# Weights repacked in load order, and the last expert pair of a two-layer MoE trunk summed in PSUM

## The chip, the core and the metric

The kernel runs on one core of one Trainium2 chip. The metric is device time in microseconds (us) of one execution. Engines are named PE (TensorE), DVE (VectorE), ACT (ScalarE), POOL (GpSimd) and SP (SyncE, which here only issues DMAs). All times in the text are from one profiled execution unless it says otherwise.

## What is computed

A trunk of two layers over 256 tokens of width 1024, all in float32. Each layer has a mixer sub-layer and a mixture of 32 experts, both modulated by six vectors that a matrix `w_ada` makes out of one conditioning vector; a final RMS norm ends it. Cut to what matters here:

```python
mod = silu(c) @ w_ada[l] + b_ada[l]                  # sh1, sc1, g1, sh2, sc2, g2
h = modulate(rms_norm(x, mixer_norm_g[l]), sh1, sc1)
x = x + g1 * (mixed(h @ w_in[l]) @ w_out[l])         # conv and pooling branches inside
h2 = modulate(rms_norm(x, ffn_norm_g[l]), sh2, sc2)  # top-1 group, top-2 experts in it
for e in range(32):                                  # combine[:, e] is 0 for tokens not routed to e
    act = silu(h2 @ w_gate[l, e]) * (h2 @ w_up[l, e])
    x = x + g2 * ((act * combine[:, e]) @ w_down[l, e])
return rms_norm(x, final_norm_g)
```

Each weight is read once: 296 MB in all, 201 MB of it the experts' (3 MB an expert).

## The kernel before

**Weights.** `plan` writes a list of 1 MB tiles in the order of their use; `issue` walks it and lets SP issue the DMAs, in that order. A tile goes into one of 14 ring buffers (`wt`, 128 partitions x 2048 floats), or into one of up to five work buffers (`wx`, table `SPARE`) while these are not needed for other things. Each `done(key)` in the program frees a buffer and plans the next load, which waits on the chip until the buffer's last reader is through. Besides, the framework hands out eight semaphores (DMAHW0 to DMAHW7) to the DMAs of SP and ACT in turn, in the order in which the program names the DMAs: a DMA cannot be issued before the one eight places ahead of it has landed. So at most eight are under way, whatever their size.

**How a tile is read.** A `w_in` tile lies packed in DRAM and is one DMA of 1 MB, 8 KB a partition. The others are read out of the tables as the caller has them: a gate/up tile is two DMAs of 512 KB, one from the gate table and one from the up table, 4 KB a partition (L112); a tile of `w_expert_down`, `w_ada`, `w_out` or `w_conv_out` is one DMA of 1 MB in runs of 4 KB (L114); the down tiles of the last pair of a layer are two DMAs of 512 KB each.

**Experts.** `blocks` goes through 16 pairs of experts; a pair has up to 64 tokens for each expert, and the two experts stand beside each other in the 128 partitions. A pair needs six tiles: four of gate/up (key `("gu", l, expert, h)`, h being the half of the contraction) and two of down (`("ed", l, expert)`). On PE a pair is, in order: gate/up, 32 matmul instructions (L1118); the previous pair's results scattered back to the 256 tokens (`scatter`, four parts of two matmuls, L1073 and L1074, three parts ahead of the transposes and one behind); two transposes (L1133); down, 16 instructions in two halves of 512 output columns (`down`, L1093). ACT takes silu (L1126), which stands once in each pair, DVE multiplies by the routing weight (L1127) and evacuates the transposes (L1135). Then, for each half, DVE multiplies by g2 (`gain`, L1099), ACT rounds this to the short format fp32r (L1100), and DVE makes the remainder (`rest`, L1104), so that two fast matmuls give full precision in the scatter. `add` (L1081) adds a scattered part from PSUM to the token array `xs` on DVE.

**The gain of the final norm** is loaded in the second layer: at the end of pair 5 (counted from 0) ACT issues a 4 KB DMA into the tile `fz` (L1204), and after pair 9 two matmuls spread it over the partitions (L1208).

**The end.** After the last pair's down, its parts are scattered and added like the others, ACT takes the squares of `xs` (L340), POOL multiplies the left half by the gain (L1180) and takes the power -1/2 (L346), ACT and DVE scale (L1214, L1215), and SP issues four output DMAs one after the other (L1218).

## Time and profile before

| | us |
|---|---|
| median of 3 runs (lowest, highest) | 851.8 (851.02, 852.24) |
| the profiled execution, its own time | 852.07 |
| its span, first to last event of the profile | 850.2 |

The page of the profile gives PE as busy for 778.5 us, 92% of the span, and the DMA queue of SP as 89.6% of 16 DMA engines over it. Neither says which of the two is waited for: matmuls overlap in their records, and the DMA queue is often full ahead of need. That is read from the distance of one pair to the next, from the GB/s of stretches, and from the waits.

### The profile page before, as it was taken

Reading aid. Unit: us, or ns where it says so; the run is one execution under the profiler, and the core shown is the slowest. Engines: PE = TensorE matmul, PEld = TensorE weight load, DVE = VectorE, ACT = ScalarE, POOL = GpSimd, SP = SyncE. Lnnn points to the kernel's source line nnn. Section 1 sums busy time; section 2 is a strip of 40 time slices with the busy share of each in tenths; the row PEclk is TensorE's granted clock in tenths of the full one; section 3 lists DMA queues with packets and bytes.
Section 4 is the critical chain, followed back from the end, with each engine's and each line's share of the span. In section 5 each row is a group of like instructions: output and inputs, shape, how many; then the busy total and the mean of one; then the engine's idle time right before and its main releaser. Section 6 shows DMA issues by size and latency. Waiting matters only on the chain. (4 is left out here: it accounts for less than half of the span.)

```text
span 850.2 us, 11978 instructions
## 1 busy us (share of the span) xinstructions
PE 778.5 (92%) x4382; PEld 454.4 (53%) x4382; DVE 505.6 (59%) x1023; ACT 277.0 (33%) x494; POOL 198.2 (23%) x133
## 2 busy tenths in 40 slices
PE   4599999997899999999879999999779999999985
PEld 2389986755333433343349998686523333333432
DVE  2369984976344644545376997497734554544545
ACT  2254544434122222222145454543322222222212
POOL 1258972510000000000034898161000000000001
PEclk9699999999999999999989999999889999999998
DMA  9999758969999999999999954797579998999993
GB/s 358 413 421 411 270 174 333 358 238 403 393 409 408 409 410 402 409 409 409 403 417 420 381 182 149 293 385 256 193 264 366 409 405 316 408 410 408 409 408 119
DMA packets 78080, 298.39 MB, mean 351 GB/s; under 512 B 7349, under 2 KB 7861, under 8 KB 74426
## 3 DMA queue, kind: packets, MB, share of 16 engines
q1 hardware_dynamic: 77448, 296.44, 89.6%
q10 hardware_dynamic: 434, 1.06, 0.3%
q8 instruction: 37, 0.61, 0.3%
q14 instruction: 33, 0.27, 0.1%
q0 software_dynamic: 128, 0.02, 0.0%
HBM read 296.44 MB, written 1.05 MB: 350 GB/s over the span
## 5 line engine op out<-in xcount | busy, mean ns | idle before, releaser
L1118 PE MATMUL pb<-wt,XTW 128*64 128x512 f32 x872 | 219.6, 593 | 12.9 <-DMA wt<-in_w_expert_up_dram 8.2
L414 POOL TENSOR_TENSOR wlo<-wt,whi 128x1024 fp32r<-128x1024 f32 x60 | 147.3, 2466 | 88.5 <-ACT whi L412 64.8
L1118 PEld LDWEIGHTS pb<-wt,XTW 128*64 128x64 f32 x872 | 73.6, 137 | 131.3 <-issue 124.5
L1127 DVE SCALAR_TENSOR_TENSOR sl<-sl,rtile,pb 128x256 f32<-128x256 f32 x32 | 15.4, 480 | 164.4 <-ACT sl L1126 164.4
L473 DVE SCALAR_TENSOR_TENSOR pd<-vpad,cols,pd 128x256 f32<-128x256 f32 x232 | 106.9, 488 | 5.7
L412 ACT CAST whi<-wt 128x1024 fp32r<-128x1024 f32 x80 | 82.8, 1049 | 73.8 <-PE pb L352 40.8
L1093 PE MATMUL pd<-wt,aT 128*64 128x512 f32 x360 | 102.7, 618 | 1.8 <-DVE aT L1135 0.5
L1100 ACT CAST yhl<-y 128x512 fp32r<-128x512 f32 x64 | 39.6, 619 | 137.9 <-DVE y L1099 137.9
L351 PE MATMUL pa<-hhl,whi 128*128 128x256 f32 x224 | 66.7, 298 | 5.2 <-ACT hhl L386 5.2
L1126 ACT ACTIVATE sl<-pb 128x256 f32<-128x256 f32 x32 | 12.3, 385 | 172.7 <-PE pb L1118 172.7
L352 PE MATMUL pa<-hhl,whi 128*128 128x256 f32 x224 | 65.6, 293 | 0.3
L353 PE MATMUL pa<-hhl,wlo 128*128 128x256 f32 x224 | 64.5, 288 | 0.6 <-POOL wlo L414 0.6
L351 PE MATMUL pb<-hhl,whi 128*128 128x256 f32 x224 | 63.6, 284 | 0.0
L297 PE MATMUL pd<-wt,cb 128*32 128x512 f32 x384 | 51.4, 623 | 13.1 <-DMA wt<-in_w_ada_dram 13.0
L352 PE MATMUL pb<-hhl,whi 128*128 128x256 f32 x224 | 62.7, 280 | 0.0
L353 PE MATMUL pb<-hhl,wlo 128*128 128x256 f32 x224 | 62.6, 279 | 0.0
L1093 PEld LDWEIGHTS pd<-wt,aT 128*64 128x64 f32 x360 | 29.1, 141 | 59.4 <-issue 39.2
L1104 DVE TENSOR_TENSOR yhl<-y,yhl 128x512 fp32r<-128x512 f32 x64 | 44.3, 693 | 22.0 <-ACT yhl L1100 22.0
L392 POOL MEMSET vpad<- 128x120 f32 x2 | 0.4, 200 | 242.5 <-DVE sl L1127 242.5
L1118 PE MATMUL pb<-wx,XTW 128*64 128x512 f32 x152 | 55.1, 593 | 0.0
L1093 PE MATMUL pd<-wx,aT 128*64 128x512 f32 x152 | 52.7, 610 | 0.8 <-DVE aT L1135 0.5
L1099 DVE TENSOR_TENSOR y<-pd,gb 128x512 f32<-128x512 f32 x64 | 44.0, 688 | 15.4 <-PE pd L1093 15.4
(257 smaller groups left out, 1345.5 us busy)
## 6 DMA issues: line engine op xcount, KB each, us to landing
wt<-in_w_expert_gate_dram SPq DMA_DIRECT2D x109, 512.0 KB, 11.5
wt<-in_w_expert_up_dram SPq DMA_DIRECT2D x109, 512.0 KB, 12.8
wt<-in_w_ada_dram SPq DMA_DIRECT2D x48, 1024.0 KB, 13.7
wt<-in_w_expert_down_dram SPq DMA_DIRECT2D x41, 1024.0 KB, 11.7
wt<-in_w_in_dram SPq DMA_DIRECT2D x28, 1024.0 KB, 20.1
wx<-in_w_expert_down_dram SPq DMA_DIRECT2D x19, 1024.0 KB, 12.0
wx<-in_w_expert_gate_dram SPq DMA_DIRECT2D x19, 512.0 KB, 11.1
wx<-in_w_expert_up_dram SPq DMA_DIRECT2D x19, 512.0 KB, 10.2
```

Of the source, the lines that this page charges most:

```text
L297: nc.tensor.matmul(ps[j:j + 32, :], cb[:, 2 * i + a, :], halves(w[:, a, :], h), start=i == 0, stop=i == 3)
L351: nc.tensor.matmul(o, ah, bh, start=start, stop=False, skip_group_check=True)
L352: nc.tensor.matmul(o, ah, bl, start=False, stop=False, skip_group_check=True)
L353: nc.tensor.matmul(o, al, bh, start=False, stop=stop, skip_group_check=True)
L412: nc.scalar.copy(hi, wv)
L414: eng.tensor_tensor(lo, wv, hi.bitcast(F32), op=OP.subtract)
L473: nc.vector.scalar_tensor_tensor(acc[:, j, :] if t == CONV_K - 1 else a, src, w, a, op0=OP.mult, op1=OP.add)
L1093: nc.tensor.matmul(o[64 * j:64 * j + 64, :], aTs[b][:, h, 64 * j:64 * j + 64], wv[j][:, h, :], start=h == 0, stop=h == 1)
L1099: nc.vector.tensor_tensor(y, downs.pop(n), s["g2"][:, n * 512:(n + 1) * 512], op=OP.mult)
L1100: nc.scalar.copy(ys[b][0][:, n * 512:(n + 1) * 512], y)
L1104: nc.vector.tensor_tensor(yl, downs.pop(("y", n)), yh.bitcast(F32), op=OP.subtract)
L1118: nc.tensor.matmul(p[64 * j:64 * j + 64], XT[:, k, 64 * j:64 * j + 64], w[j][:, :, kk, :], start=k == 0, stop=k == KC - 1)
```

## The change

The host lays out all weights as 1 MB tiles in load order, each contiguous, 8 KB a partition: `w_gate_up` puts the gate and the up rows of a tile behind each other, `w_down`, `w_ada`, `w_out` and `w_conv_out` are packed likewise. Every tile is then one DMA. In the last pair of each layer the two gate/up tiles of h = 1 hold contraction steps 4, 5 and 6, 7 of both experts, in the place of one expert each. In the last pair of layer 1, ACT first copies `xs` into four PSUM tiles (`hold`), and the scatters of the last two pairs are accumulated on them by PE (`onto`), those of the pair before between the two halves of gate/up; the second half of the last down is done in two pieces of 256 columns whose results are scattered as plain float32, without the split into fp32r and remainder. The final norm reads PSUM (`last` takes the place of `finish`), and one of the four output DMAs is issued by ACT.

```diff
-            key, src, (a, b), q = stream[state["issued"]]
+            key, src, shape, q = stream[state["issued"]]
             t = room(key, q)
             if t is None:
                 return
-            v = t[:, :a * b].rearrange("p (a b) -> p a b", b=b)
-            if isinstance(src, tuple):
-                v = v.rearrange("p (i k) h -> p i k h", i=2)
-                for i, sr in enumerate(src):
-                    nc.sync.dma_start(out=v[:, i], in_=sr)
-            else:
-                nc.sync.dma_start(out=v, in_=src)
+            v = t[:, :src.shape[-1]]
+            nc.sync.dma_start(out=v, in_=src)
+            v = v.rearrange(*(("p (a b) -> p a b",) if len(shape) == 2 else ("p (i a b) -> p i a b",)),
+                            **dict(zip("ab" if len(shape) == 2 else "iab", shape)))
             tiles[key] = v
...
     def plan_ada(l, m, part=range(4)):
-        v = w_ada[l].rearrange("(p k) n -> p k n", k=KC)
         for i in part:
-            plan(("ada", l, m, i), v[:, 2 * i:2 * i + 2, m * D:(m + 1) * D], (2, D))
+            plan(("ada", l, m, i), w_ada[l, m, i], (2, D))
 
...
     def plan_pair(l, e):
-        ents = []
-        for h in range(2):
-            for j in range(2):
-                ents.append((("gu", l, e + j, h),
-                             tuple(w[l, e + j].rearrange("(p k) h -> p k h", k=KC)[:, 4 * h:4 * h + 4, :]
-                                   for w in (w_expert_gate, w_expert_up)), (KC, DE)))
-        wd = w_expert_down[l, e:e + 2].rearrange("e (j p) n -> p e j n", p=P)
-        for j in range(2):
-            if e + 2 < NE:
-                ents.append((("ed", l, e + j), wd[:, j], (2, D)))
-            else:
-                ents.append((("ed", l, e + j), tuple(wd[:, z, :, 512 * j:512 * j + 512] for z in range(2)), (4, 512)))
+        ents = [(("gu", l, e + j, h), w_gate_up[l, e + j, h], (4, 2, DE) if h and e + 2 == NE else (2, 4, DE))
+                for h in range(2) for j in range(2)]
+        ents += [(("ed", l, e + j), w_down[l, e + j], (2, D) if e + 2 < NE else (2, 2, 512)) for j in range(2)]
...
+        def gate_up(b, p, XT, h):
+            w = need(*(("gu", l, 2 * b + j, h) for j in range(2)))
+            for kk in range(4):
+                k = 4 * h + kk
+                for j in range(2):
+                    wv = w[kk // 2][:, 2 * j:2 * j + 2, kk % 2, :] if h and b == nb - 1 else w[j][:, :, kk, :]
+                    nc.tensor.matmul(p[64 * j:64 * j + 64], XT[:, k, 64 * j:64 * j + 64], wv,
+                                     start=k == 0, stop=k == KC - 1)
+                if h and b == nb - 1 and kk % 2:
+                    done(("gu", l, 2 * b + kk // 2, h))
+            if not (h and b == nb - 1):
+                for j in range(2):
+                    done(("gu", l, 2 * b + j, h))
+
+        sums = {}
+
+        def hold():
+            for h in range(2):
+                for tt in range(TT):
+                    t = sums[h, tt] = ((pa, pa), (pd, pb))[h][tt]([P, 512])
+                    nc.scalar.copy(t, xs[:, tt, h * 512:(h + 1) * 512])
+
+        def onto(h, tt, G, y, c=slice(0, 512)):
+            G = G[:, tt, :]
+            if y.dtype == F32:
+                G = G.bitcast(F32)
+            else:
+                y = y[:, h * 512:(h + 1) * 512]
+            nc.tensor.matmul(sums[h, tt][:, c], G, y, start=False, stop=True, skip_group_check=True)
+
...
+                fin = l + 1 == DEPTH and b == nb - 1
+                if fin:
+                    hold()
+                gate_up(b, p, XT, 0)
+                if fin:
+                    for h in range(2):
+                        for tt in range(TT):
+                            onto(h, tt, GTs[b - 1], ys[b - 1][0])
+                            onto(h, tt, GTs[b - 1], ys[b - 1][1])
+                gate_up(b, p, XT, 1)
                 if b == 0:
                     spread(r)
                     prep(0)
                 sl = moe.tile([P, DE], F32, name="sl", bufs=1)
                 nc.scalar.activation(sl, p[:, 0, :], AF.Silu)
                 nc.vector.scalar_tensor_tensor(sl, sl, r["ws"][:, b:b + 1], p[:, 1, :], op0=OP.mult, op1=OP.mult)
-                for part in range(3):
-                    scatter(b - 1, part)
-                add(b - 1, 0)
+                if not fin:
+                    for part in range(3):
+                        scatter(b - 1, part)
+                    add(b - 1, 0)
                 q = pt([P, 2, P])
                 for h in range(2):
                     nc.tensor.transpose(q[:, h, :], sl[:, h * P:(h + 1) * P], ident)
                 aTs[b] = moe.tile([P, 2, P], F32, name="aT", bufs=1)
                 nc.vector.tensor_copy(aTs[b], q)
-                scatter(b - 1, 3)
+                if not fin:
+                    scatter(b - 1, 3)
                 window(b + 1)
-                for part in range(1, 4):
+                for part in range(1, 0 if fin else 4):
                     add(b - 1, part)
...
+            if l + 1 == DEPTH:
+                return last(b)
...
+        def last(b):
+            xn = work.tile([P, TT, D], F32, name="xn", tag="X0")
+            junk = work.tile([P, D], F32, name="junk", tag="bigA")
+            ss = [two.tile([P, 2], F32, name="ss") for _ in range(TT)]
+            h0, h1 = slice(0, 512), slice(512, 1024)
+            down(b, 0)
+            done(("ed", l, 2 * b))
+            wd, = need(("ed", l, 2 * b + 1))
+            os = [f([P, 256]) for f in (pd, pt)]
+            for z in range(2):
+                cs = slice(256 * z, 256 * z + 256)
+                for h in range(2):
+                    for j in range(2):
+                        nc.tensor.matmul(os[z][64 * j:64 * j + 64, :], aTs[b][:, h, 64 * j:64 * j + 64], wd[:, j, h, cs],
+                                         start=h == 0, stop=h == 1)
+            gain(b, 0)
+            yc = two.tile([P, 512], F32, name="y", tag="part", bufs=3)
+            for z in range(2):
+                cs = slice(256 * z, 256 * z + 256)
+                nc.vector.tensor_tensor(yc[:, cs], os[z], s["g2"][:, 512 + 256 * z:768 + 256 * z], op=OP.mult)
+                if z == 0:
+                    rest(b, 0)
+            for q in range(2):
+                for tt in range(TT):
+                    onto(0, tt, GTs[b], ys[b][q])
+            for z in range(2):
+                cs = slice(256 * z, 256 * z + 256)
+                for tt in range(TT):
+                    onto(1, tt, GTs[b], yc[:, cs], cs)
+            sq = float(D) ** -0.5
+            for tt in range(TT):
+                nc.scalar.activation(junk[:, h0], sums[0, tt], AF.Square, scale=sq, accum_out=ss[tt][:, 0:1])
+                nc.vector.tensor_tensor(xn[:, tt, h0], sums[0, tt], fin_g["b"][:, h0], op=OP.mult)
+            for tt in range(TT):
+                nc.scalar.activation(junk[:, h1], sums[1, tt], AF.Square, scale=sq, accum_out=ss[tt][:, 1:2])
+            rss = [rms_scale(tt, ss[tt]) for tt in range(TT)]
+            for tt in range(TT):
+                nc.scalar.activation(xn[:, tt, h0], xn[:, tt, h0], AF.Identity, scale=rss[tt])
+                nc.vector.scalar_tensor_tensor(xn[:, tt, h1], sums[1, tt], rss[tt], fin_g["b"][:, h1],
+                                               op0=OP.mult, op1=OP.mult)
+                for z, hs in enumerate((h0, h1)):
+                    (nc.scalar if tt > z else nc.sync).dma_start(out=out[0, tt * P:(tt + 1) * P, hs], in_=xn[:, tt, hs])
+            return xn, rss
...
+    v = a["w_ada"].reshape(DEPTH, P, 4, 2, 6, D).transpose(0, 4, 2, 1, 3, 5)
+    r["w_ada"] = v.reshape(DEPTH, 6, 4, P, 2048)
+    for k in ("w_conv_out", "w_out"):
+        r[k] = a[k].reshape(DEPTH, -1, 2, P, D).transpose(0, 1, 3, 2, 4).reshape(DEPTH, -1, P, 2048)
+    gu = np.stack([a[k].reshape(DEPTH, NE, P, 2, 4 * DE) for k in ("w_expert_gate", "w_expert_up")], 4)
+    gu = np.ascontiguousarray(gu.transpose(0, 1, 3, 2, 4, 5)).reshape(DEPTH, NE, 2, P, 2048)
+    for q in range(2):
+        ks = slice(4 + 2 * q, 6 + 2 * q)
+        v = np.stack([a[k].reshape(DEPTH, NE, P, KC, DE)[:, z, :, ks] for z in (NE - 2, NE - 1)
+                      for k in ("w_expert_gate", "w_expert_up")], 2)
+        gu[:, NE - 2 + q, 1] = v.reshape(DEPTH, P, 2048)
+    r["w_gate_up"] = gu
+    v = a["w_expert_down"].reshape(DEPTH, NE, 2, P, D).transpose(0, 1, 3, 2, 4)
+    wd = np.ascontiguousarray(v).reshape(DEPTH, NE, P, 2048)
+    for n in range(2):
+        wd[:, NE - 2 + n] = v[:, NE - 2:, :, :, 512 * n:512 * n + 512].transpose(0, 2, 1, 3, 4).reshape(DEPTH, P, 2048)
+    r["w_down"] = wd
```

On SP, around the load of the final gain, `order` of the program before shows the following; the names are the tile and its source, and DMAHWn is the semaphore that the DMA eight places ahead in the program has raised. The gain's DMA, on ACT's queue, stands in the program behind the second row and has DMAHW1; the last row but one is the next to have that semaphore.

```order
L112 DMA wt_11622<-in_w_expert_gate_dram 128x1024 [waits DMAHW7_49,PE_49]
L112 DMA wt_11622<-in_w_expert_up_dram 128x1024 [waits DMAHW0_49]
L112 DMA wt_11625<-in_w_expert_gate_dram 128x1024 [waits DMAHW2_49,PE_49]
L112 DMA wt_11625<-in_w_expert_up_dram 128x1024 [waits DMAHW3_49]
L112 DMA wt_11636<-in_w_expert_gate_dram 128x1024 [waits DMAHW4_49,PE_49]
L112 DMA wt_11636<-in_w_expert_up_dram 128x1024 [waits DMAHW5_49]
L112 DMA wt_11639<-in_w_expert_gate_dram 128x1024 [waits DMAHW6_49,PE_49]
L112 DMA wt_11639<-in_w_expert_up_dram 128x1024 [waits DMAHW7_49]
L114 DMA wt_11712<-in_w_expert_down_dram 128x2x1024 [waits DMAHW0_49,PE_49]
L114 DMA wx_11714<-in_w_expert_down_dram 128x2x1024 [waits DMAHW1_49,PE_49]
L112 DMA wx_11725<-in_w_expert_gate_dram 128x1024 [waits DMAHW2_49,PE_49]
```

In the changed program it stands behind the first of these rows and has DMAHW2, which the last row but one has next. In both programs the row ahead of it is of the same weight tile.

```order
L109 DMA wt_11560<-in_w_gate_up_dram 128x2048 [waits DMAHW1_49,PE_49]
L109 DMA wt_11562<-in_w_gate_up_dram 128x2048 [waits DMAHW3_49,PE_49]
L109 DMA wt_11572<-in_w_gate_up_dram 128x2048 [waits DMAHW4_49,PE_49]
L109 DMA wt_11574<-in_w_gate_up_dram 128x2048 [waits DMAHW5_49,PE_49]
L109 DMA wt_11646<-in_w_down_dram 128x2048 [waits DMAHW6_49,PE_49]
L109 DMA wx_11648<-in_w_down_dram 128x2048 [waits DMAHW7_49,PE_49]
L109 DMA wx_11659<-in_w_gate_up_dram 128x2048 [waits DMAHW0_49,PE_49]
L109 DMA wt_11661<-in_w_gate_up_dram 128x2048 [waits DMAHW1_49,PE_49]
L109 DMA wt_11671<-in_w_gate_up_dram 128x2048 [waits DMAHW2_49,PE_49]
L109 DMA wt_11673<-in_w_gate_up_dram 128x2048 [waits DMAHW3_49,PE_49]
```

What moved: between the gain's load and the DMA that waits for it lay four tiles in seven DMAs, and now lie seven tiles in seven DMAs.

On PE, at the last pair of layer 1, the program before has these rows, from the down of the pair before (pair 14) to its own (L1118 is gate/up, L1073 and L1074 the scatter, L1133 the transposes, L1093 down):

```order
L1093 MATMUL pd<-wt,aT 64x512 x8
L1118 MATMUL pb<-wt,XTW 64x512 x16
L1073 MATMUL pa<-yhl,GT 128x512
L1074 MATMUL pa<-yhl,GT 128x512
L1073 MATMUL pa<-yhl,GT 128x512
L1074 MATMUL pa<-yhl,GT 128x512
L1073 MATMUL pd<-yhl,GT 128x512
L1074 MATMUL pd<-yhl,GT 128x512
L1133 MATMUL pt<-idc,sl 128x128 x2
L1073 MATMUL pd<-yhl,GT 128x512
L1074 MATMUL pd<-yhl,GT 128x512
L1093 MATMUL pd<-wt,aT 64x512 x8
```

The changed program, from the gate/up of the last pair to the end (L1108 is gate/up, L1130 the scatter onto PSUM, L1161 the transposes, L1089 and L1228 down):

```order
L1108 MATMUL pb<-wt,XTW 64x512 x8
L1130 MATMUL pa<-yhl,GT 128x512 x4
L1130 MATMUL pd<-yhl,GT 128x512 x2
L1130 MATMUL pb<-yhl,GT 128x512 x2
L1108 MATMUL pb<-wt,XTW 64x512 x8
L1161 MATMUL pt<-idc,sl 128x128 x2
L1089 MATMUL pd<-wt,aT 64x512 x4
L1228 MATMUL pd<-wt,aT 64x256 x4
L1228 MATMUL pt<-wt,aT 64x256 x4
L1130 MATMUL pa<-yhl,GT 128x512 x4
L1130 MATMUL pd<-y,GT 128x256
L1130 MATMUL pb<-y,GT 128x256
```

What moved: the scatter of pair 14, eight matmuls, stands between the halves of gate/up and no longer behind them, and four scatter matmuls of 256 columns in plain float32 take the place of four of 512 in fp32r. On all engines but SP the rows ahead of the last pair of layer 1 are the same in both programs, apart from a path for overflowing experts that these inputs don't take.

## Rows read from the trace of the kernel before

**Rows 1.** Windows: stretch, its length, each engine busy, granted clock, DMA busy share, GB/s.

```profile
40.00:70.00 30.00, 29.39 (x244) 26.38 (x244) 19.39 (x32) 14.18 (x16) 20.29 (x9) 0.97 1.01 419
440.00:470.00 30.00, 27.74 (x208) 25.17 (x209) 21.21 (x34) 15.30 (x19) 15.96 (x9) 0.89 1.01 420
222.00:422.00 200.00, 192.69 (x855) 75.11 (x856) 98.67 (x179) 46.25 (x106) 0.00 (x0) 0.99 1.03 408
590.00:600.00 10.00, 5.15 (x42) 3.12 (x41) 9.17 (x36) 1.81 (x2) 0.52 (x1) 0.89 1.01 361
642.00:694.00 52.00, 51.81 (x238) 19.98 (x236) 26.70 (x48) 12.30 (x28) 0.95 (x1) 1.00 1.02 397
694.00:706.00 12.00, 11.95 (x56) 4.67 (x54) 6.68 (x12) 3.06 (x7) 0.00 (x0) 1.00 0.75 282
706.00:834.00 128.00, 123.45 (x541) 49.14 (x538) 61.08 (x110) 28.92 (x66) 0.00 (x0) 1.00 1.01 400
```

**Rows 2.** DMA issues: KB each, us from issue to landing.

```profile
wt<-in_w_expert_gate_dram SPq DMA_DIRECT2D x109, 512.0 KB, 11.5
...
wt<-in_w_in_dram SPq DMA_DIRECT2D x28, 1024.0 KB, 20.1
```

**Rows 3.** Timeline of ACT, layer 0: start, us, and idle time before.

```profile
379.52 0.39 ACT L1126 ACTIVATE sl<-pb 128x256 f32<-128x256 f32 x1 [5.23 <-PE pb L1118]
...
394.60 0.39 ACT L1126 ACTIVATE sl<-pb 128x256 f32<-128x256 f32 x1 [7.46 <-PE pb L1118]
...
409.94 0.39 ACT L1126 ACTIVATE sl<-pb 128x256 f32<-128x256 f32 x1 [7.69 <-PE pb L1118]
...
425.45 0.39 ACT L1126 ACTIVATE sl<-pb 128x256 f32<-128x256 f32 x1 [7.85 <-PE pb L1118]
```

**Rows 4.** Timeline of ACT, layer 1, the silu of four pairs.

```profile
786.87 0.39 ACT L1126 ACTIVATE sl<-pb 128x256 f32<-128x256 f32 x1 [5.23 <-PE pb L1118]
...
801.86 0.38 ACT L1126 ACTIVATE sl<-pb 128x256 f32<-128x256 f32 x1 [7.37 <-PE pb L1118]
...
817.22 0.38 ACT L1126 ACTIVATE sl<-pb 128x256 f32<-128x256 f32 x1 [7.71 <-PE pb L1118]
...
832.59 0.39 ACT L1126 ACTIVATE sl<-pb 128x256 f32<-128x256 f32 x1 [7.72 <-PE pb L1118]
```

**Rows 5.** Timeline of SP, around the gain's load.

```profile
693.64 0.38 SPq L114 DMA_DIRECT2D wt<-in_w_expert_down_dram  x1
703.47 0.38 SPq L114 DMA_DIRECT2D wx<-in_w_expert_down_dram  x1
```

**Rows 6.** Waits of SP: us in total, times, longest.

```profile
SPq L114 <- DMA fz<-in_final_norm_g_dram: 9.4, 1, 9.4
```

**Rows 7.** Timeline of ACT in layer 1, the gain's load.

```profile
701.94 0.49 ACTq L1204 DMA_DIRECT2D fz<-in_final_norm_g_dram  x1
```

**Rows 8.** Timeline of PE at the start.

```profile
27.54 1.69 PE L297 MATMUL pd<-wt,cb 128*32 128x512 f32 x8 [1.48 <-DMA wt<-in_w_ada_dram]
```

**Rows 9.** Chain that ended last: start, us, what.

```profile
832.55 0.43 PE pa L1073
832.98 0.23 PE pa L1074
...
834.89 1.96 PE pd L1093 x8
```

**Rows 10.** Timeline of the end.

```profile
838.30 0.69 DVE L1104 TENSOR_TENSOR yhl<-y,yhl 128x512 fp32r<-128x512 f32 x1 [0.74 <-ACT yhl L1100]
...
842.29 0.63 ACT L340 ACTIVATE xn<-xs 128x512 f32<-128x512 f32 x1
...
843.77 1.06 POOL L346 TENSOR_TENSOR rs<-sm,mhalf 128x1 f32<-128x1 f32 x2
...
845.10 1.82 SPq L1218 DMA_DIRECT2D out_dram<-xn  x4
```

**Rows 11.** Timeline of PE in layer 0: plain float32, 256 columns.

```profile
221.94 1.11 PE L977 MATMUL pd<-dg,ones 128*128 128x256 f32 x4
```

More of the change, by code (lines that the diff above doesn't have):

```diff
@@ L51, in trunk @@
 def trunk(ctx, tc, x, c, w_ada, b_ada, w_in, ada_cols, mix_rows, router, pool_w, w_conv_out, w_out,
-          w_expert_gate, w_expert_up, w_expert_down, final_norm_g, out):
+          w_gate_up, w_down, final_norm_g, out):
     nc = tc.nc
@@ L1010, in overflow @@
                     p = pa([P, 2, DE])
-                    for i, wsrc in enumerate((w_expert_gate, w_expert_up)):
-                        wv = wsrc[l, e].rearrange("(p k) h -> p k h", k=KC)
+                    for i in range(2):
                         for h in range(2):
                             w = wsp.rearrange("p (k h) -> p k h", h=DE)
-                            nc.gpsimd.dma_start(out=w, in_=wv[:, 4 * h:4 * h + 4, :])
+                            if h and e >= NE - 2:
+                                o = (2 * (e - NE + 2) + i) * 2 * DE
+                                for q in range(2):
+                                    nc.gpsimd.dma_start(out=wsp[:, 2 * q * DE:2 * (q + 1) * DE],
+                                                        in_=w_gate_up[l, NE - 2 + q, 1, :, o:o + 2 * DE])
+                            else:
+                                nc.gpsimd.dma_start(out=wsp, in_=w_gate_up[l, e, h, :, 4 * DE * i:4 * DE * (i + 1)])
                             for kk in range(4):
@@ L1029, in overflow @@
                     for h in range(2):
-                        nc.gpsimd.dma_start(out=wsp, in_=w_expert_down[l, e].rearrange("(j p) n -> p j n", p=P)[:, h])
+                        if e < NE - 2:
+                            nc.gpsimd.dma_start(out=wsp, in_=w_down[l, e, :, D * h:D * (h + 1)])
+                        else:
+                            z = (2 * (e - NE + 2) + h) * 512
+                            for n in range(2):
+                                nc.gpsimd.dma_start(out=wsp[:, n * 512:(n + 1) * 512],
+                                                    in_=w_down[l, NE - 2 + n, :, z:z + 512])
                         for n in range(2):
@@ L1112, in blocks @@
                 XT = XTW[b % 2]
-                for h in range(2):
-                    w = need(*(("gu", l, 2 * b + j, h) for j in range(2)))
-                    for kk in range(4):
-                        k = 4 * h + kk
-                        for j in range(2):
-                            nc.tensor.matmul(p[64 * j:64 * j + 64], XT[:, k, 64 * j:64 * j + 64],
-                                             w[j][:, :, kk, :], start=k == 0, stop=k == KC - 1)
-                    for j in range(2):
-                        done(("gu", l, 2 * b + j, h))
+                fin = l + 1 == DEPTH and b == nb - 1
[8 more added lines that the diff above has]
+                gate_up(b, p, XT, 1)
                 if b == 0:
```

25 lines of the change are left out of this document (7 added, 18 removed).

## Prediction

> **What bounds the kernel now.** I read the windows of GB/s first, then the silu rows of ACT, since silu stands once in each pair, then the waits of SP, and the chain and the timeline for the end.
>
> The windows [rows 1] show two speeds of one busy DMA queue. Where SP loads `w_in`, the stretches 40 to 70 and 440 to 470, it moves 419 and 420 GB/s; where it loads experts, 222 to 422, it moves 408, with a DMA busy share above 1 in all three. What differs is the row that a DMA reads: a gate DMA of 512 KB over 128 partitions has rows of 4 KB, a `w_in` DMA of 1 MB has 8 KB [rows 2]. The two DMAs differ too in how long they are under way, 11.5 and 20.1 us: eight may be out, which is some 5 MB in one case and 8 MB in the other.
>
> A full queue need not be waited for. ACT idles 5.23 us before the silu of a pair that waits for nothing; before the last three of layer 0 it idles 7.46, 7.69 and 7.85 [rows 3], before the last three of layer 1 7.37, 7.71 and 7.72 [rows 4]. A pair that the DMA paces takes 15.4 us (801.86 to 817.22, say), which is what six tiles of 1.05 MB need at 408 GB/s; without the 2.5 of extra idle it would take the 12.9 that PE needs. So in each layer PE works off the lead that the buffers gave it, and only the last three pairs wait for weights:
> - layer 0: 2.23 + 2.46 + 2.62 = 7.3 us
> - layer 1: 2.14 + 2.48 + 2.49 = 7.1 us
>
> This is all that faster loads can give there; behind it PE is the bound. The mixers don't wait for weights, apart from the start, where PE waits for each of the first `w_ada` tiles, the last time 1.48 us for the eighth [rows 8].
>
> In layer 1 there is a hole in the stream. SP stands from 693.64 to 703.47 [rows 5], and 9.4 us of that is the load of the final gain [rows 6]: the next DMA needs its semaphore, and ACT issues it only at 701.94, in its place behind pair 5 [rows 7]. The window 694 to 706 moves 282 GB/s, and the one from 706 to 834 400 [rows 1]; at 408 they would have needed (408 - 282) / 408 x 12 = 3.7 us and 2.5 us less.
>
> The end: the last gate/up matmul ends at 832.55, down begins at 834.89 [rows 9], the span ends at 850.2. That is 17.6 us of short steps on PE, DVE, ACT, POOL and SP, each waiting for the one before.
>
> **The change, part by part.** The sum is made against the profiled execution, 852.07 us; the median is 851.8, and I take the gains off that.
>
> *Packed tiles.* All weights now come as `w_in` does: 1 MB contiguous, one DMA, 8 KB a partition. I take 420 GB/s for all; the bounds are 408 (nothing gained) and 421, what the first 22 us of those windows hardly exceed.
> - Start: eight `w_ada` tiles, 8.4 MB, 20.6 us at 408, 20.0 at 420: -0.6.
> - Layer 0: between 222 and 422, 81.6 MB are loaded; at 420 that is 194.3 us instead of 200: -5.7 of the 7.3 waited. The rest, 1.6, stays before the last pair, unless small dips within the 408 go as well; the bounds are 0 and -7.3.
> - Layer 1: from 642 to 834, 52 x 397 + 12 x 282 + 128 x 400 make 75.2 MB. At 420 without the hole this is 179 us instead of 192, 13 earlier. With the old rate and no hole it is 184.3, 7.7 earlier; with the hole and the new rate, 5.5 earlier. Only 7.1 can be taken: -7.1, and at the least -5.5. The hole should close, since seven tiles instead of four lie between the gain's load and the DMA that waits for it: 3 x 2.5 = 7.5 us more work in the queue against the 3.7 us that ran dry. The gain's own wait, for the DMA eight places ahead of it, reaches further back in bytes now, so it is met earlier.
>
> [...] The windows put 8 KB rows 2.9% ahead of 4 KB rows [rows 1]. [...]
>
> SP issues a little over half as many DMAs. It was never late by its own work: its issues took 0.38 us and it waited between them [rows 5], so this is worth nothing, and would be worth nothing either way while DMA or PE is behind.
>
> *Pair 14's scatter ahead of the last half of gate/up.* Its eight matmuls take 0.43 + 7 x 0.23 = 2.04 us [rows 9]. Before, they covered silu, multiply and transposes: down began 2.34 us behind gate/up. Now nothing covers these: silu 0.39 [rows 4], a multiply of the same 256 columns, taken at 0.5, then what stood between the sixth scatter matmul and down, 2.34 - 0.43 - 5 x 0.23 = 0.76, and some 0.2 of handovers: 1.9. If PE is the bound, as I expect once the tiles are early, down begins 2.04 + 1.9 - 2.34 = +1.6 later. If the DMA is still late at this pair, the scatter and half of the h = 1 matmuls run before the last gate/up tile lands, and down begins up to 4.0 earlier: 2.04, and 1.96 for eight instructions at the price of a half of down [rows 9]. Queued behind on ACT and DVE there is nothing but this pair.
>
> *hold.* Four ACT copies of 512 columns into PSUM: no such row; the nearest is an ACT pass of 512 columns, 0.63 [rows 10], so 2.5 us. ACT idles 5.23 to 7.72 us before this silu [rows 4], which covers it. Without that cover 2.5 us would delay silu; nothing is the lower bound.
>
> *The end from down on,* counted from down's start, D. Before, D is 834.89 and the end 15.3 later.
> - The left half's chain is the old one: its eight matmuls 1.96 [rows 9], gain, rounding, remainder, which ended at 838.99, D + 4.1 [rows 10]. Meanwhile PE does the right half in two pieces, done by D + 3.7.
> - Two scatter matmuls on the remainder, then the four of 256 columns in plain float32. Their nearest row has two such matmuls in 1.11 us with start and end [rows 11], 0.43 each: they end near D + 6.5. The second round of rounding and remainder and the four adds on DVE are gone.
> - The first 128 tokens' second square, 0.63, ends near D + 6.9. Before, that square ended at 842.92 and the kernel 7.3 us later; POOL's power, which needs only a sum of 0.2 first, began at 843.77 [rows 10], since POOL had its products with the gain before it, and now has none: 0.65 less. The four output issues, 1.82 us in a row on SP [rows 10], are split between two queues: some 0.5 less. That leaves 6.1.
> - So D + 13.0: -2.3. With the +1.6 ahead of it, -0.7; bounds +1.5 (each new PSUM pass a third dearer, no gain in issue) and -3 (the DMA still binds and the early scatter helps).
>
> Sum: -0.6 - 5.7 - 7.1 - 0.7 = -14.1, so 851.8 - 14.1 = 837.7.
>
> **The rivals.**
> [...]
> 2. *The rate does not rise at all:* `w_in` is fast for another reason, such as what else goes on in that stage. For it: both fast stretches lie in the same stage of a layer. Against it: PE, DVE and ACT are busier there than with the experts, not less. Then only the hole closes, 7.7 us of DMA time, enough for the 7.1: -7.1 - 0.7 = -7.8: 844.0. [...]
> 3. *The packed layout is slower than the old one.* [...] For it: a busy queue can be slow, 361 GB/s at a share of 1.01 in 590 to 600 [rows 1]. Against it: `w_in` has just this layout. Layer 0's 81.6 MB and layer 1's 75.2 MB are read in 392 us now, so below 156.8 / 392 = 400 GB/s the kernel is slower; at 361 they take 434 us, and the end comes near 851.8 + 42 - 1 = 893.
> 4. *The change has all of it:* no wait left in layer 0 (-7.3 instead of -5.7), and an end better by 1.6: 834.5.
>
> **How the numbers follow.** The forecast has 0.67, rival 4 0.10, rival 1 0.09, rival 2 0.10, rival 3 0.04. A measurement of this kernel tells some 0.2%, 1.7 us, from no change. All but rival 3 end beyond that: faster 0.94, slower 0.04, and 0.02 of rival 2's chance for an end that also goes wrong by several us. [...] That gives 835 to 840; taking in the neighbours down to rival 4 and up to rival 1 and most of rival 2, 834 to 843.5.
>
> **What would show it.** Expert stretches at 418 to 421 GB/s; landing near 20 us for all tiles; ACT's idle time before silu back at 5.2 in all pairs of layer 1 and in at least two of the last three of layer 0; no stand of SP at the gain's load; the last down 1.9 us behind the end of gate/up, and the end 13 us behind down. It is wrong if the expert stretches stay at 408, if pairs 13 to 15 still idle 7.4 or more, or if the accumulation on PSUM makes PE or ACT wait at the last pair.

## The result, and the profile after

The changed kernel takes 837.12 us (median; 835.61 to 839.28), the kernel before 851.41 beside it: ratio 0.984, 95% interval 0.9807 to 0.9872, 14.3 us less. The forecast was 837.7, 14.1 less. The profiled execution took 835.61 us, its span is 833.8 (before 850.2), 16.4 less.

The windows of the changed kernel, the stretches of [rows 1] as far as they still mean the same work (columns as there; the one behind 706 ends at 800, while the DMA queue still has weights to load):

```profile
40.00:70.00 30.00, 29.70 (x253) 26.90 (x254) 21.51 (x35) 14.47 (x16) 21.14 (x10) 1.00 1.01 419
440.00:470.00 30.00, 30.00 (x257) 28.40 (x256) 22.84 (x41) 13.13 (x15) 21.14 (x10) 1.00 1.01 419
222.00:422.00 200.00, 197.93 (x889) 76.16 (x889) 102.68 (x186) 46.08 (x106) 0.20 (x1) 0.99 1.01 420
640.00:694.00 54.00, 53.81 (x248) 20.73 (x246) 28.14 (x51) 12.84 (x29) 0.95 (x1) 1.00 1.01 421
694.00:706.00 12.00, 11.95 (x58) 4.68 (x56) 6.31 (x12) 3.07 (x7) 0.00 (x0) 1.00 0.86 341
706.00:800.00 94.00, 93.61 (x422) 36.62 (x420) 47.09 (x85) 22.43 (x51) 0.00 (x0) 1.00 1.01 422
```

The experts now load at 420 to 422 GB/s, the rate that `w_in` had before. The stretch behind the gain's load is still the slow one, 341. From issue to landing a gate/up tile in a ring buffer takes 15.9 us and a down tile 18.5 (8.3 and 12.5 in the work buffers), so the sign "near 20 us for all tiles" did not show. The timeline of ACT, the silu of the last four pairs of each layer (answers to [rows 3, 4]; start, us, idle time before) and between them the load of the final gain (answer to [rows 7]):

```profile
377.05 0.38 ACT L1153 ACTIVATE sl<-pb 128x256 f32<-128x256 f32 x1 [5.23 <-PE pb L1108]
...
389.90 0.39 ACT L1153 ACTIVATE sl<-pb 128x256 f32<-128x256 f32 x1 [5.23 <-PE pb L1108]
...
402.75 0.38 ACT L1153 ACTIVATE sl<-pb 128x256 f32<-128x256 f32 x1 [5.23 <-PE pb L1108]
...
415.58 0.38 ACT L1153 ACTIVATE sl<-pb 128x256 f32<-128x256 f32 x1 [5.20 <-PE pb L1108]
...
692.26 0.49 ACTq L1275 DMA_DIRECT2D fz<-in_final_norm_g_dram  x1
...
777.24 0.39 ACT L1153 ACTIVATE sl<-pb 128x256 f32<-128x256 f32 x1 [5.23 <-PE pb L1108]
790.09 0.38 ACT L1153 ACTIVATE sl<-pb 128x256 f32<-128x256 f32 x1 [5.23 <-PE pb L1108]
802.91 0.38 ACT L1153 ACTIVATE sl<-pb 128x256 f32<-128x256 f32 x1 [5.20 <-PE pb L1108]
817.97 0.38 ACT L1153 ACTIVATE sl<-pb 128x256 f32<-128x256 f32 x1 [5.37 <-PE pb L1108]
```

The idle time is 5.2 before seven of these and 5.37 before the last: none of these pairs waits for a load, in either layer. Of the distances only the last is long, 15.06 us where 12.85 is the rule; that is the scatter which now stands ahead of half of gate/up. ACT issues the gain's load in the same place as before, behind pair 5, and SP's wait for it [rows 6] has grown. SP's waits (us in total, times, longest):

```profile
SPq L109 <- DMA fz<-in_final_norm_g_dram: 13.9, 1, 13.9
```

The chain that ended last, from the last gate/up on (start, us, what; answers to [rows 9]):

```profile
808.85 3.43 PE pb L1108 x16
812.28 1.14 PE pa L1130 x4
813.42 0.46 PE pd L1130 x2
813.88 0.46 PE pb L1130 x2
814.34 3.61 PE pb L1108 x16
818.39 0.49 DVE sl L1154
818.93 0.45 PE pt L1161 x2
819.88 1.94 PE pd L1089 x8
```

and the timeline of the end (answers to [rows 10]):

```profile
826.11 0.60 ACT L1249 ACTIVATE junk<-pd 128x512 f32<-128x512 f32 x1
...
827.13 0.55 POOL L331 TENSOR_TENSOR rs<-sm,mhalf 128x1 f32<-128x1 f32 x1 [182.96 <-DVE sm L329]
...
828.47 1.31 SPq L1256 DMA_DIRECT2D out_dram<-xn  x3
829.18 0.38 ACTq L1256 DMA_DIRECT2D out_dram<-xn  x1
```

Divided at the silus of ACT, the two profiled executions differ like this (all in us):

| stretch | before | after | difference |
|---|---|---|---|
| start to the first silu of layer 0 | 223.57 | 221.32 | -2.25 |
| first to second silu of layer 0 | 14.61 | 14.40 | -0.21 |
| second to last silu of layer 0 | 187.27 | 179.86 | -7.41 |
| to the first silu of layer 1 | 202.10 | 203.43 | +1.33 |
| first to second silu of layer 1 | 15.86 | 14.77 | -1.09 |
| second silu to that of pair 14 | 173.81 | 169.13 | -4.68 |
| pair 14 to pair 15 | 15.37 | 15.06 | -0.31 |
| last silu to the end of the span | 17.61 | 15.83 | -1.78 |

Four stretches (lines 1, 2, 4, 5) hold no wait of an expert pair for a load; together they give -2.2. The rest gives -14.2.

### The profile page after: what moved, and what is told of

The parts are those of the page before. It is cut to its first block, busy times and chain, and to the rows that moved or that the text cites. A ratio compares the mean times of both kernels' runs of the same rounds, so it can differ in the third digit from the quotient of the medians.

```text
span 833.8 us, 11862 instructions
## 1 busy us (share of the span) xinstructions
PE 772.6 (93%) x4394; PEld 452.6 (54%) x4394; DVE 499.9 (60%) x1017; ACT 278.1 (33%) x497; POOL 196.5 (24%) x131
## 5 line engine op out<-in xcount | busy, mean ns | idle before, releaser
L1108 PE MATMUL pb<-wt,XTW 128*64 128x512 f32 x872 | 215.2, 597 | 5.3 <-ACT XTW L1052 2.8
L1108 PEld LDWEIGHTS pb<-wt,XTW 128*64 128x64 f32 x872 | 70.0, 138 | 122.2 <-issue 116.2
L1089 PE MATMUL pd<-wt,aT 128*64 128x512 f32 x352 | 99.9, 614 | 2.2 <-DVE aT L1163 1.0
L331 POOL TENSOR_TENSOR rs<-sm,mhalf 128x1 f32<-128x1 f32 x10 | 7.6, 757 | 230.3 <-DVE sm L329 230.3
L1089 PEld LDWEIGHTS pd<-wt,aT 128*64 128x64 f32 x352 | 28.4, 140 | 57.6 <-issue 37.6
L1108 PE MATMUL pb<-wx,XTW 128*64 128x512 f32 x152 | 55.1, 594 | 0.0
L1089 PE MATMUL pd<-wx,aT 128*64 128x512 f32 x152 | 52.5, 609 | 0.8 <-DVE aT L1163 0.5
## 6 DMA issues: line engine op xcount, KB each, us to landing
wt<-in_w_gate_up_dram SPq DMA_DIRECT2D x109, 1024.0 KB, 15.9
wt<-in_w_down_dram SPq DMA_DIRECT2D x45, 1024.0 KB, 18.5
wx<-in_w_down_dram SPq DMA_DIRECT2D x19, 1024.0 KB, 12.5
```

What stands on the lines that cost most here:

```text
L1089: nc.tensor.matmul(o[64 * j:64 * j + 64, :], aTs[b][:, h, 64 * j:64 * j + 64], wv[j][:, h, :], start=h == 0, stop=h == 1)
L1108: nc.tensor.matmul(p[64 * j:64 * j + 64], XT[:, k, 64 * j:64 * j + 64], wv, start=k == 0, stop=k == KC - 1)
```

## The experiments

The kernel before ran beside each group, at 851.4 to 852.1 us. "Waits in layer 0" below is the time from the second to the last silu above the 179.86 of the changed kernel, in which no pair waits; by this measure the kernel before has 7.4 us. In the edits, `...` marks rows left out, and rows that only fit other parts to the edit are not shown.

**The two halves of the change alone.** All weights packed, with the end of the kernel before:

```diff
-                fin = l + 1 == DEPTH and b == nb - 1
+                fin = False
...
-            if l + 1 == DEPTH:
-                return last(b)
```

> All weights packed, the end of the kernel before (scatter of pair 14 behind gate/up, adds into xs, finish). Theory: the loads are early in the last pair, so the new end gives back at gate/up (2.04 us of scatter with nothing to hide behind it, measured 15.06 us for that pair against 12.85) what it saves behind it (last silu to the end 15.83 us against 17.61): about 0.4 us less than the changed kernel, 836.7 us, with 12.85 us from silu to silu in the last pair and 17.6 us from the last silu to the end. Rival, the prediction's own term: the new end is worth 0.7 us, so 837.8 us.

Measured: 837.82 us, ratio 0.9834 (0.9815 to 0.9853). The last pair takes 12.86, last silu to end 17.8; from the silu of pair 14 to the end 30.7 us against 30.9 in the changed kernel. So the new end is worth nothing that can be told where the loads are early: by the stretch, 0.2 us, the sign is the theory's; the median, 837.8, is the rival's and not the 836.7 of the theory, but two sets of runs of the changed kernel differ by more than these two (837.12 and 837.99).

The loads of the kernel before with the new end (`issue`, `plan_ada`, `plan_out` and `plan_pair` as before, except):

```diff
+                if h and e + 2 == NE:
+                    ents.append((("gu", l, e + j, h), w_gate_up[l, e + j, h], (4, 2, DE)))
+                    continue
```

> The loads of the kernel before in tables and sizes, with the new end; only the two h = 1 gate/up tiles of the last pair of each layer come packed, as their arrangement needs. Theory: here the loads are late (waits of about 7 us before the last three pairs in each layer, as in the kernel before), so the scatter and half of the h = 1 matmuls run while the last tile is still under way: down begins about 2.2 us earlier, and the end is 1.4 us shorter: 847.8 us. By the prediction's bound down begins up to 4.0 us earlier: 846 us. Rival: the new end is worth nothing by itself, 851.4 us.

Measured: 848.21 us, ratio 0.995 (0.993 to 0.997). The size is right and the place is not. From the silu of pair 14 to down it takes 17.80 us, before 17.67: down begins no earlier. Its chain:

```profile
820.35 4.25 PE pb L1127 x16
824.60 1.13 PE pa L1149 x4
825.73 0.46 PE pd L1149 x2
826.19 0.46 PE pb L1149 x2
826.66 3.61 PE pb L1127 x16
```

Behind the scatter nothing waits for a tile: the second half of gate/up takes 3.61 us, as in the changed kernel. By the time the scatter is done, the late tiles have landed; it fills the time that the arrangement by contraction steps would have saved. From down to the end it is 13.9 us against 15.3: -1.4. The rest came in layer 0, where the arrangement stands without a scatter in its way: the last pair takes 13.61 us there, before 15.51. Another 1.1 us came there ahead of the arrangement, at pair 13; two profiles with the old loads and without the arrangement differ by 0.7 (waits of 7.4 and 8.1 us), so that may be no more than executions differ by.

**The scatter's place.**

```diff
                 gate_up(b, p, XT, 0)
-                if fin:
-                    for h in range(2):
-                        for tt in range(TT):
-                            onto(h, tt, GTs[b - 1], ys[b - 1][0])
-                            onto(h, tt, GTs[b - 1], ys[b - 1][1])
                 gate_up(b, p, XT, 1)
...
+                for part in range(3):
+                    if fin:
+                        onto(*divmod(part, 2), GTs[b - 1], ys[b - 1][0])
+                        onto(*divmod(part, 2), GTs[b - 1], ys[b - 1][1])
```

and the fourth part behind the transposes.

> The changed kernel with one thing put back: the eight scatter matmuls of pair 14 stand behind gate/up again (six ahead of the transposes, two behind), still summed in PSUM. Theory: with early loads they are best used to cover silu, multiply and transposes: the last silu comes 2.0 us earlier, down begins 2.3 us behind gate/up in place of 1.96, 1.6 us less in all: 835.5 us. Rival: PE has the same work either way and the place does not matter, 837.1 us.

Measured: 836.47 us, ratio 0.9819 (0.9799 to 0.9838). From the silu of pair 14 to the end 29.06 us against 30.9: -1.8, as the theory has it, though whole times cannot tell this alone.

**What sets the rate.** Each packed tile in two DMAs with rows of 4 KB:

```diff
-            nc.sync.dma_start(out=v, in_=src)
+            n = src.shape[-1] // 2
+            for z in range(2):
+                nc.sync.dma_start(out=v[:, z * n:z * n + n], in_=src[:, z * n:z * n + n])
```

> The changed kernel with each packed tile read in two DMAs of 512 KB over 128 partitions, each with rows of 4 KB. Theory (the row's size sets the rate): 406 to 410 GB/s in the expert stretch of layer 0 in place of 420, and waits of 5 to 7 us in all before its last three pairs; 848 to 852 us. Rival (one contiguous megabyte a tile sets the rate, whatever the rows): 418 to 421 GB/s, no waits there, 837 us. A low rate here does not yet tell rows of 4 KB from twice the number of DMAs; the same tiles in two DMAs of 64 partitions with rows of 8 KB will.

Measured: 851.06 us, ratio 0.9984 (0.9963 to 1.0005): all of the gain is gone. Its windows:

```profile
40.00:70.00 30.00, 29.16 (x249) 26.16 (x248) 19.95 (x33) 14.12 (x15) 21.15 (x10) 1.00 1.03 409
...
222.00:422.00 200.00, 194.02 (x866) 75.54 (x867) 99.56 (x185) 46.23 (x106) 0.00 (x0) 0.99 1.03 409
...
694.00:706.00 12.00, 11.95 (x56) 4.28 (x54) 6.45 (x12) 2.67 (x6) 0.00 (x0) 1.00 0.57 197
```

`w_in` falls from 419 to 409 as well. Waits in layer 0: 4.8 us. The hole behind the gain's load is deeper than in the kernel before, 197 GB/s for 282.

To tell the rows from the number of DMAs, rows of 8 KB in two DMAs of 64 partitions:

```diff
-            nc.sync.dma_start(out=v, in_=src)
+            for z in range(2):
+                nc.sync.dma_start(out=v[64 * z:64 * z + 64], in_=src[64 * z:64 * z + 64])
```

> The changed kernel with each packed tile read in two DMAs of 512 KB as in e4_rows_4k, but each over 64 partitions with rows of 8 KB. Theory (row size): 418 to 421 GB/s in the expert stretch of layer 0, no waits before its last three pairs, 837 to 839 us. Rival (twice the DMAs, and 4 MB under way where 8 were, set the rate): 406 to 410 GB/s, 848 to 852 us.

Measured: 1149.7 us, ratio 1.336 (1.328 to 1.344). Neither had this. The window of the first `w_in` tiles:

```profile
40.00:70.00 30.00, 16.30 (x94) 9.28 (x94) 6.73 (x13) 5.77 (x9) 4.71 (x2) 0.69 1.02 220
```

220 GB/s, a little over half of 419, with a busy share of 1.02; in 222 to 422 it is 254. The same with even and odd partitions:

```diff
+            for z in range(2):
+                nc.sync.dma_start(out=v[z::2], in_=src[z::2])
```

> As e5_parts_8k, two DMAs of 512 KB a tile with rows of 8 KB, but one over the even and one over the odd partitions. [...] Theory B (e5 was slow because 64 rows are too few for 16 DMA engines, 4 each): 220 to 270 GB/s as there, some 1150 us.

Measured: 865.8 us, ratio 1.017 (1.014 to 1.0201). The rate is not the 220 to 270 GB/s of theory B but 419 and 416, beside 419 and 420 in the changed kernel; the time is not the changed kernel's:

```profile
40.00:70.00 30.00, 29.61 (x252) 26.82 (x253) 20.85 (x36) 14.43 (x16) 21.43 (x10) 1.00 1.01 419
...
222.00:422.00 200.00, 196.85 (x888) 98.45 (x886) 98.98 (x181) 46.23 (x106) 0.00 (x0) 0.99 1.01 416
...
694.00:706.00 12.00, 11.95 (x57) 6.05 (x54) 6.68 (x12) 3.06 (x7) 0.00 (x0) 1.00 0.01 2
```

No pair of layer 0 waits (each takes 12.92 us where 12.85 is the rule). In layer 1 SP stands 26.7 us for the gain's load; with 4 MB under way the stream runs dry for most of it, and from pair 7 on all pairs but one are late:

```profile
SPq L110 <- DMA fz<-in_final_norm_g_dram: 26.7, 1, 26.7
```

Its span is 28.7 us longer than that of the changed kernel, and 16.5 of it lie here, from the second silu of layer 1 to that of pair 14. Another 10.2 lie in the start and the mixers, which the expectation does not name; their cause stays open.

And one DMA a tile, whose rows are 4 KB (the two expert tables stored in two blocks a tile):

```diff
+                nc.sync.dma_start(out=v.rearrange("p (z n) -> p z n", z=2), in_=src.rearrange("z p n -> p z n"))
```

> The changed kernel with each expert tile still one DMA of one contiguous megabyte, but stored as two blocks of 512 KB, so that a partition's 8 KB are two runs of 4 KB. The other tables stay as they are. Theory (row size): 406 to 410 GB/s in the expert stretch of layer 0, waits of 4 to 5 us before its last three pairs, 843 to 850 us. Rival (number of DMAs or bytes under way): 418 to 421 GB/s, 837 us.

Measured: 838.35 us, ratio 0.9853 (0.9816 to 0.9891). The rate is that of the theory, the time nearly that of the rival:

```profile
40.00:70.00 30.00, 29.31 (x250) 26.51 (x250) 21.26 (x35) 14.21 (x15) 21.15 (x10) 1.00 1.02 420
222.00:422.00 200.00, 195.93 (x872) 75.72 (x871) 99.45 (x181) 46.62 (x107) 0.20 (x1) 0.99 1.03 409
...
694.00:706.00 12.00, 11.95 (x56) 4.68 (x54) 5.83 (x12) 2.69 (x7) 0.00 (x0) 1.00 1.00 380
```

In one kernel `w_in`, with rows of 8 KB, goes at 420 and the experts, with 4 KB, at 409. Together with two DMAs a tile of 4 KB rows (409) and two of 8 KB rows over every second partition (419 and 416) this settles the rate: it goes with the row, not with the number of DMAs nor the bytes under way. But waits in layer 0 are only 2.9 us, and there are none in layer 1. The silus of the last two pairs of layer 0:

```profile
406.79 0.38 ACT L1157 ACTIVATE sl<-pb 128x256 f32<-128x256 f32 x1 [7.13 <-PE pb L1112]
...
420.64 0.38 ACT L1157 ACTIVATE sl<-pb 128x256 f32<-128x256 f32 x1 [6.20 <-PE pb L1112]
```

The same without the arrangement by contraction steps:

```diff
-                    wv = w[kk // 2][:, 2 * j:2 * j + 2, kk % 2, :] if h and b == nb - 1 else w[j][:, :, kk, :]
+                    wv = w[j][:, :, kk, :]
```

> The kernel of e6_one_dma_4k (rows of 4 KB at 409 GB/s, one DMA a tile) without the arrangement by contraction steps: the last h = 1 tiles of both layers hold one expert each, like the others. Theory: where the loads are late, half of the h = 1 matmuls waits for the second tile, so in layer 0 the last pair goes from 13.85 to 15.3 to 15.7 us and the waits before its last three pairs from 2.9 to 4.8 us; in layer 1 the tiles are there and nothing changes: 840 us. Rival (the arrangement is worth nothing, the lead alone cut the waits): the last pair of layer 0 stays at 13.9 us, 838.4 us.

Measured: 840.36 us, ratio 0.9868 (0.9841 to 0.9896). The last pair of layer 0 takes 15.31 us in place of 13.85; waits in layer 0 are 3.8 us, not 4.8, since the pair ahead of it waited less:

```profile
408.64 0.38 ACT L1154 ACTIVATE sl<-pb 128x256 f32<-128x256 f32 x1 [6.57 <-PE pb L1112]
...
423.95 0.38 ACT L1154 ACTIVATE sl<-pb 128x256 f32<-128x256 f32 x1 [7.67 <-PE pb L1112]
```

**The gain's load.** The kernel before, and the changed one, with the load on POOL's queue:

```diff
-            nc.scalar.dma_start(out=fin_g["row"][0:1, :], ...
+            nc.gpsimd.dma_start(out=fin_g["row"][0:1, :], ...
```

> The kernel before with one word changed: the load of the final gain is issued by POOL on its own queue and not by ACT, so no DMA of SP waits for its semaphore. Theory: SP's stand of 9.4 us goes, the stretch 694 to 706 moves 400 GB/s in place of 282, the stream is some 6 us ahead from there on, and of the 7.1 us that layer 1's last three pairs wait about 1 is left: 845.5 to 846.5 us. Rival: the stream catches up anyway, or another wait takes its place: 851 to 852 us.

Measured: 846.19 us, ratio 0.9933 (0.9909 to 0.9956), as the theory had it. The kernel before, so edited: the window that moved 282 GB/s, and the silus of the last three pairs, of which one still waits.

```profile
694.00:706.00 12.00, 11.95 (x56) 4.83 (x56) 6.68 (x12) 3.06 (x7) 0.00 (x0) 1.00 1.03 409
```

```profile
799.26 0.38 ACT L1126 ACTIVATE sl<-pb 128x256 f32<-128x256 f32 x1 [5.23 <-PE pb L1118]
812.09 0.38 ACT L1126 ACTIVATE sl<-pb 128x256 f32<-128x256 f32 x1 [5.21 <-PE pb L1118]
826.55 0.38 ACT L1126 ACTIVATE sl<-pb 128x256 f32<-128x256 f32 x1 [6.82 <-PE pb L1118]
```

> The same word in the changed kernel. There SP stands 13.9 us for the gain, longer than before. Theory: the stand costs the stream some 2 us, but the last pair's tiles land 5 us or more ahead of their use, so the time stays: 837 us, with all pairs of layer 1 at 12.85 us as they are. Rival: the stand still costs its share, 2 us or more: 835 us.

Measured: 836.86 us, ratio 0.982 (0.9791 to 0.985). The window 694 to 706 rises from 341 to 420 GB/s, and from the silu of pair 14 to the end it stays 30.9 us: the hole costs the changed kernel nothing.

**Both edits together, and the changed kernel again.**

> The changed kernel with both edits that the runs so far speak for: pair 14's scatter behind gate/up, still summed in PSUM, and the gain's load on POOL's queue. Theory: 1.6 us less than the changed kernel run beside it for the scatter, nothing for the gain: from the silu of pair 14 to the end of the span 29.05 us against 30.9. Rival: no difference between the two.

> The changed kernel once more, unaltered, beside e11 on the same chip: 837 us, 30.9 us from the silu of pair 14 to the end of the span. It also shows how far the first silu of layer 0 moves between two executions of one program: 221.3 us in the first profile of this kernel, 223.7 to 225.2 in three others whose program is the same up to there. If that is chance, any value from 221 to 226; if the packed w_ada made the 221.3, that value again.

Measured: 834.84 us (ratio 0.9799, 0.9775 to 0.9822) and 837.99 us (0.9836, 0.9812 to 0.986). From the silu of pair 14 to the end of the span: 29.05 and 30.9 us, both as expected. Of the 3.2 us between the medians 1.85 is thus placed; the rest is no more than two executions of one program differ by. The first silu of layer 0 came at 221.45 and 223.68: chance.

## Why the prediction was right, point by point

The whole came out within 1 us. The parts did not all: layer 0 gave 1.7 us more than its term and the end 1.1 less, and that these nearly cancel is luck.

**Rate: right.** 420 was the value taken, 420 to 422 it is. In the kernel whose two kinds of rows run side by side it is 420 GB/s for rows of 8 KB and 409 for rows of 4, 2.7%. No run shows a smaller rise, for which rival 1 has its 0.09. And the thought that `w_in` is fast for its stage falls: with rows of 4 KB it falls to 409 there.

**Layer 0: mis-sized, and put on one cause where three work.** The term was -5.7 "of the 7.3 waited", all of it from the rate, with 1.6 left over. It is -7.4, with nothing left. And the rate of the experts is not needed for most of it: at the old 409, one DMA a tile (with the smaller tables packed) cuts the waits from 7.4 (8.1 in the profile of the kernel before with the edited gain) to 3.8, the arrangement in the last pair cuts them to 2.9, and only the rest is the rows' when they come last. They are not additive: with two DMAs a tile and the arrangement, rows of 8 KB remove all 4.8 (in that kernel the mixers take longer too). So rival 2, no gain in rate at all, would have ended near 838.4 and not at the 844.0 that the prediction gave it: it let layer 0 keep its 7.3.

What the prediction put at nothing is the number of DMAs: "worth nothing, and would be worth nothing either way". SP's own work is indeed not the limit, but eight DMAs of 512 KB are half the bytes of eight of 1 MB. Two kernels whose experts both load at 409 GB/s, with two DMAs a tile and with one, take 851.06 and 838.35 us (the first has 4 KB rows in the other tables too); from the second to the changed kernel, 409 to 420, it is only 1.2 us less, within what executions differ by. Part of this the traces can place. When the buffers come free again ahead of the experts, SP waits for earlier DMAs to land if a tile is two DMAs, and for engines alone if it is one. From 190 to 235 its waits for DMAs add up to 15.7 us with two DMAs of 4 KB rows, and with one there are none. The largest of SP's waits for a DMA there with two, and the largest of all with one (us in total, times, longest):

```profile
SPq L111 <- DMA wt<-in_w_gate_up_dram: 9.4, 11, 0.9
```

```profile
SPq L110 <- PE pd L1093: 10.7, 1, 10.7
```

Up to the first silu of layer 0 the kernel with two has moved 337 GB/s x 225.65 us = 76.0 MB, the one with one 344 x 223.29 = 76.8. The 0.8 MB are a lead of 2.0 us at 409 GB/s, and 1.9 is what their waits differ by (4.8 and 2.9). The kernel before and the same with the edited gain have moved 76.0 and 75.9 MB up to there, the one with one DMA and no arrangement 76.9; these 0.9 to 1.0 MB are some 2.3 us, a little over half of the 3.6 and 4.2 by which the waits differ. The rest stays open, and so does what of it is due to the smaller tables; no run changed the stretch ahead of the experts alone.

**Layer 1: right in size, half right in its reason.** All 7.1 us of waits are gone. "The hole should close" and "no stand of SP at the gain's load" were wrong: SP stands 13.9 us instead of 9.4, since it runs further ahead of ACT, which issues the load in its place behind pair 5. What I had right is why it matters less: with 8 MB under way the stretch moves 341 GB/s, not 282, a loss of (420 - 341) / 420 x 12 = 2.3 us in place of 3.7. In the kernel before, the hole was nearly the whole cause of layer 1's waits: with it gone and the old rate, 1.6 of 7.1 us is left. In the changed kernel it is covered. With 4 MB under way and rows of 8 KB it is not (2 GB/s); with 4 MB and rows of 4 KB (197) no run separates the hole from the rate.

**The end: wrong in sign, -0.7 for +0.4.** From the second silu of layer 1 to the end the term was -7.8, and -6.8 came. Ahead of down the +1.6 is +1.8: the last pair is 2.2 us longer than 12.85, and down then begins 1.91 behind the silu instead of 2.30. The "some 0.2 of handovers" in the term was an estimate that no row showed; in the chain of the changed kernel PE to ACT takes 0.02, ACT to DVE 0.04 and DVE to PE 0.05 us up to the transposes. From down's start D to the end -2.3 was forecast and -1.4 came, 13.9 us for 13.0. Up to the first 128 tokens' second square the forecast holds (D + 6.8 for D + 6.9). The step that failed is "some 0.5 less" for splitting the output issues over two queues, together with the 0.65 for POOL. POOL starts 0.4 sooner behind the square, not 0.65. The issues are indeed done 2.65 us behind POOL's start in place of 3.15. But from the first of them to the end of the span it is 5.3 us, before 5.1, and the first issue stands as far behind POOL's start as ever (1.34 us, before 1.33). So the issue of the last was not what the end waited for; what is left is the landing of the 1 MB that the four carry, which no run took apart.

The bound "down begins up to 4.0 earlier" where the loads are late was wrong as well, by the old loads with the new end: 0.1 later. The 2.04 of scatter had been covering silu, so taking it from there saves little, and put ahead of h = 1 it takes the time that the arrangement frees.

**Start and mixers: -0.6 forecast, -2.2 in the profile, too scattered to judge.** The four stretches without waits add up to 452.2 to 456.2 us in six profiles of programs that are the same up to there but for the gain's load, mean 454.6, and to 455.0 to 456.4 in three with the old loads, mean 455.8. The -1.2 between the means is within that scatter, so neither -0.6 nor nothing at all is excluded. The range of 835 to 840 has in it 1 to 2 us either way for PE's clock, my estimate; no run shows this term. What the runs show in its place are two profiles whose programs are the same up to the first silu: one spends 6.8 us more at the lower granted clock in two windows, and its first silu comes 2.23 us later (last section).

## What to carry to other kernels

Where a stream of loads starts with a lead and loses a little at every step, what counts is at which step the lead ends: once enough was gained from any one side, the rest is worth nothing (here, of layer 0's waits, rows of 8 KB remove all 4.8 us with two DMAs a tile, and one DMA a tile with the arrangement 4.5 of 7.4 at the old rate), so single gains must not be added, and each cause must be tried without the others. Where only so many DMAs may be under way, their number counts beside the rate: with the experts at 409 GB/s both times, one DMA a tile in place of two came with some 12 us less. A DMA of another queue that shares semaphores with the weight stream stops it for as long as its own engine is behind, here SP for 9.4 us before and 13.9 after; put it on a queue of its own (that stretch rose from 282 to 409 GB/s, and from 341 to 420), or keep enough bytes under way to cover the stop. Work that covers a chain of short steps on other engines must not be moved ahead of that chain once the engine that does it is the bound: here it was worth 1.8 us to put the scatter back.

## What the runs showed of the hardware

In the window 40 to 70 DMAs over 64 neighbouring partitions move 220 GB/s, DMAs over every second of the 128 419, with the same rows, sizes and number under way; in 222 to 422 it is 254 and 416. 220 / 419 is 0.53 and 254 / 416 is 0.61, with a DMA busy share of 1.01 to 1.02 in all four windows. What makes the neighbours slower was not shown.

The same program can differ by 4 us between executions: the second set of runs of the changed kernel lies between 835.60 us, at a mean granted clock of 0.976, and 839.74, at 0.968. Where the clock falls is seen in two profiles whose programs are the same up to the first silu. Two windows (columns as in [rows 1]) of the changed kernel with both edits, whose first silu came at 221.45:

```profile
28.00:45.00 17.00, 12.08 (x78) 9.39 (x74) 7.44 (x14) 7.57 (x11) 4.72 (x2) 0.80 1.01 420
196.00:204.00 8.00, 6.20 (x40) 5.08 (x40) 3.83 (x11) 2.48 (x5) 0.00 (x0) 1.00 0.89 367
```

and of the changed kernel run beside it, with 223.68:

```profile
28.00:45.00 17.00, 12.40 (x70) 9.67 (x74) 7.50 (x14) 7.62 (x11) 4.72 (x2) 0.70 1.01 421
196.00:204.00 8.00, 5.71 (x26) 3.89 (x27) 3.32 (x8) 1.53 (x3) 0.00 (x0) 0.79 0.99 408
```

In the kernel before, windows of 0.5 us from 440 to 470 have a granted clock of 1.00 or 0.50, apart from the two in which it changes (0.86 and 0.81). With these two levels, as an estimate, a mean of 0.80 over 17 us is 6.8 us at the lower one, 0.70 is 10.2, and 0.79 over 8 us 3.4; the first execution stays at the upper level in that last stretch. Together the second spends 6.8 us more at the lower level in these two windows, and its first silu comes 2.23 us later. In the kernel before, PE idles for 2.50 us up to 441.29, and the clock is 0.50 from 441.0 to 447.5. Whether such a pause brings the lower level, and which does, was not tried.

In the profile of the kernel before, one small DVE instruction near the start took 2.21 us where it takes 0.17 in the changed kernel; it ends as an instruction of POOL does, 33.5. Timeline of the kernel before, DVE and POOL:

```profile
31.14 2.34 POOL L414 TENSOR_TENSOR wlo<-wt,whi 128x1024 fp32r<-128x1024 f32 x1 [17.23 <-ACT whi L412]
31.30 2.21 DVE L330 TENSOR_TENSOR A<-A,ad 128x8 f32<-128x8 f32 x1
```

The first matmul of the mixer waits behind it. In two other profiles with the old loads this instruction takes 0.17 us and is over at 30.53 and 31.04, before POOL begins (31.20 and 31.31); the first silu came at 224.5 there all the same, later than the 223.57 here. What held the instruction for 2.21 us was not shown.
